# Merge gates as Tanh and inverse deviations as one power on GpSimd, in a hybrid retention and recurrence layer

## Chip, cores and metric

The kernel runs on one core of one Trainium2 chip. The metric is the device time of one execution in microseconds (us), lower is better. Engines are called as in the profile: PE is TensorE's matrix multiply and PEld its weight load, DVE is VectorE, ACT is ScalarE, POOL is GpSimd, SP is SyncE, which only issues transfers here.

## What is computed

One layer on 1024 rows of 1024 features, all in float32 (norm weights, biases and the small gates left out of this sketch):

```python
h = rms_norm(x, norm1_w)
q, k, v, g_ret, x_lru, y_lru, gate_ret, gate_lru = split(h @ w_in)     # 8192 columns
o = head_group_norm(chunkwise_retention(rotary(q), rotary(k), v), ret_gn_w)
y_a = (o * silu(g_ret)) @ w_ret_o
y_b = (rg_lru(conv4(x_lru)) * gelu(y_lru)) @ w_lru_o
mix = sigmoid(gate_ret + merge_gate_b[0]) * y_a + sigmoid(gate_lru + merge_gate_b[1]) * y_b
x = x + mix @ w_out
gate, val = split(rms_norm(x, norm2_w) @ ffn_w_up)                      # 2 * 3072 columns
x = x + (gelu(conv3(gate)) * val) @ ffn_w_down
return rms_norm(x, norm_f_w)
```

`rms_norm` multiplies by `rsqrt(mean(x*x) + 1e-6)`, `head_group_norm` by `rsqrt(var + 1e-6)` for each of four heads. In `rg_lru`, r and i are Sigmoids of two block products, `a = exp(-8 r softplus(-lam))`, and the input of the scan is `sqrt(1 - a*a) * i * x`.

## The kernel before

Every large product is split into three passes of a high and a low part (`split`: ACT rounds a tile to its high part, DVE subtracts for the low part), and many blocks go through a seven-product scheme in place of eight (`mm_fast`, L518), which needs sums of weight blocks and of operand blocks made on DVE. The rest goes through `mm_first` (L494 and L423), `mm_by` (L463) and `mm_std`. A PE instruction is 128x128 weights against 512 columns.

The work is a list of jobs, in the order given by `SEQ`: the projection's column groups, with merge gates (`g`), Gelu branches (`y`), the four retention heads (`h`) and recurrence inputs (`x`) mixed, then the two branch outputs (`ojobs`), `w_out` (`wjobs`), 24 up-projection jobs (`ups`) and twelve down-projection jobs (`djobs`). While a job's matmuls are issued, `pump` prepares weight blocks ahead, `build` prepares operands, and `advance` runs generators of other work (retention, recurrence, rotary tables) a little at a time. These amounts are counted in the program text. The order of instructions on each engine is made by the framework from priorities (`hp`) and from when operands should be ready, so that the small instructions of one chain stand between others.

What the change touches:

- `rstd_of` makes 1/sqrt of a few columns: a Sqrt on ACT, then on DVE a reciprocal and one Newton step of four instructions. It is called by `rms_scale` (first norm, twice with four columns), `retention_head` (eight times with four columns), `out_post` (second norm, four times with two columns) and `final` (last norm, eight times with one column). Its result scales tiles on DVE or ACT right behind it.
- `emit_gate` scales a gate by the row's 1/rms and takes the Sigmoid on ACT with the bias column of `par`, then stores it in `sg_d`. There are 32 such tiles, and SEQ places 12 of them before the first head and 20 behind the last head, among the recurrence blocks (five jobs of four tiles).
- `emit_ret_o` and `emit_lru_o` multiply a bank of the branch product (or the tile that holds it) by the gate read back from `sg_d`, 16 tiles each, and `emit_lru_o` adds the two branches.
- `lru_block` (recurrence) uses Sigmoid, Tanh, Exp and Sqrt on ACT in each half of each of its four blocks.
- `ret_out` multiplies a head's normalized output by `ret_gn_w` and the swish gate.
- ACT needs the function's table in place; a load is put ahead of an activation whose function is not in the table loaded last. Copies, Squares and Identity need no particular one.

GpSimd issues the transfers of the rotary tables and of the up-projection's results (`ff_d`), and makes four constants.

Of the kernel before, what the change touches and what calls it, by code (L numbers as in the profile page):

```python
# [13 lines left out]
F32 = mybir.dt.float32  # L14
F32R = mybir.dt.float32r
I32 = mybir.dt.int32
AF = mybir.ActivationFunctionType
ALU = mybir.AluOpType

P = 128  # L20
# [159 lines left out]
def tile_trunk_layer(ctx, tc, x, xt, positions, params, consts, normf, w_in, w_ro, w_lo,  # L180
# [32 lines left out]
    def pc(name, i):  # L213
        return par[:, PCOL[name] + i:PCOL[name] + i + 1]
# [393 lines left out]
    st = pool.tile([P, 16], F32, tag="st", name="st")  # L608
    nst = pool.tile([P, 5, 8], F32, tag="nst", name="nst")

    def rstd_of(dst, var, tmp):
        S.activation(tmp, var, AF.Sqrt)
        V.reciprocal(dst, tmp)
        V.tensor_mul(tmp, dst, dst)
        V.tensor_mul(tmp, tmp, var)
        V.tensor_scalar(tmp, tmp, -0.5, 1.5, ALU.mult, ALU.add)
        V.tensor_mul(dst, dst, tmp)

    def rms_scale(tiles, n, o=0):

        for t in range(n):
            for c in range(2):
                j = psa.get()
                if c == 0:
                    S.activation(j, tiles[t, c], AF.Square, accum_out=nst[:, c, o + t:o + t + 1])
                else:
                    V.scalar_tensor_tensor(j, tiles[t, c], 1.0, tiles[t, c], ALU.mult, ALU.mult,
                                           accum_out=nst[:, c, o + t:o + t + 1])
                psa.put(j)
        a, b, v, r, w = (nst[:, i, o:o + n] for i in range(5))  # L630
        V.tensor_add(v, a, b)
        V.tensor_scalar(v, v, 1.0 / D, EPS, ALU.mult, ALU.add)
        rstd_of(r, v, w)
        return r

    def reads(fetch, keys, ahead):
# [254 lines left out]
    def lru_block(n, xl):  # L891
        wg = []
        for g in range(2):
            wr = get()
            SY.dma_start(wr, w_gate[n, g])
            wg.append(split(wr))
            put(wr)
            yield 0.6
        carry = {}
        for h in range(2):  # L900
            xc, xs = [], []
            for m in range(2):
                ch = 2 * n + m
                c = get()
                src = xl[m, h]
                S.activation(c, src, AF.Identity, bias=pc("lru_conv_b", ch), scale=pc("lru_conv_w", 24 + ch))
                for s in (1, 2, 3):
                    yield 0.6
                    w = pc("lru_conv_w", 8 * (3 - s) + ch)
                    V.scalar_tensor_tensor(c[:, s:], src[:, :TH - s], w, c[:, s:], ALU.mult, ALU.add)  # L910
                    if h == 1:
                        V.scalar_tensor_tensor(c[:, :s], tails[:, m, 4 - s:4], w, c[:, :s], ALU.mult, ALU.add)
                if h == 0:
                    V.tensor_copy(tails[:, m, :], src[:, TH - 4:])
                put(src)
                xc.append(c)
                xs.append(split(c))
                yield 0.6
            yield from rest()
            rr, ii, th = [], [], []  # L920
            for m in range(2):
                for g, bn, dst in ((0, "lru_b_r", rr), (1, "lru_b_i", ii)):
                    ps = psa.get()
                    q = 0
                    for k in range(2):
                        cs = slice(256 * k + 128 * m, 256 * k + 128 * m + 128)
                        for a, b in PASSES:
                            PE.matmul(ps, wg[g][a][:, cs], xs[k][b], start=q == 0, stop=q == 5)  # L928
                            q += 1
                    t = get()  # L930
                    S.activation(t, ps, AF.Sigmoid, bias=pc(bn, 2 * n + m))
                    psa.put(ps)
                    dst.append(t)
                    yield 0.8
            drop(xs[0])
            drop(xs[1])
            for m in range(2):
                t = get()
                S.activation(t, rr[m], AF.Tanh, scale=lhalf[:, 2 * n + m:2 * n + m + 1])
                V.tensor_mul(ii[m], ii[m], xc[m])  # L940
                put(xc[m])
                th.append(t)
                yield 0.6
            for m in range(2):
                S.activation(rr[m], rr[m], AF.Exp, scale=lneg[:, 2 * n + m:2 * n + m + 1])
            for m in range(2):
                V.scalar_tensor_tensor(rr[m], rr[m], 1.0, th[m], ALU.add, ALU.mult)
                V.tensor_scalar(rr[m], rr[m], -1.0, 1.0, ALU.mult, ALU.add)
                yield 1.0
            for m in range(2):  # L950
                S.activation(th[m], th[m], AF.Sqrt)
            for m in range(2):
                ch = 2 * n + m
                e, i, r = rr[m], ii[m], th[m]
                y = get()
                ST.dma_start(y, y_d[ch, :, TH * h:TH * h + TH])
                V.tensor_mul(i, i, r)
                yield 0.6
                V.scalar_tensor_tensor(i, e, 1.0, i, ALU.add, ALU.mult)
                yield 0.6  # L960
                V.tensor_tensor_scan(r, e, i, 0.0 if h == 0 else carry[m], ALU.mult, ALU.add)
                if h == 0:
                    k = st[:, m:m + 1]
                    V.tensor_copy(k, r[:, TH - 1:TH])
                    carry[m] = k
                V.tensor_mul(y, y, r)
                ST.dma_start(u_d[ch, :, TH * h:TH * h + TH], y)
                put(e, i, r, y)
                yield 1.7
        for w in wg:  # L970
            drop(w)
# [35 lines left out]
    def retention_head(hd, qk, vv):  # L1007
        cur = 0
        mask = cst[:, C_MASK + 128 * hd:C_MASK + 128 * hd + 128]
        for h in range(2):  # L1010
# [48 lines left out]
                V.bn_aggr(mv[:, b, :], bst[:, b, :])  # L1059
                yield 1.5  # L1060
            V.tensor_scalar(rs[:, 0, :], mv[:, :, 1], cst[:, C_GEPS + hd:C_GEPS + hd + 1], None, ALU.add)
            rstd_of(rs[:, 1, :], rs[:, 0, :], rs[:, 2, :])
            for b in range(4):
                o = ob[h, b // 2][:, 256 * (b % 2):256 * (b % 2) + 256]
                V.tensor_scalar(o, o, mv[:, b, 0:1], rs[:, 1, b:b + 1], ALU.subtract, ALU.mult)
# [27 lines left out]
    def ret_out(hd, gg):  # L1093
        yield from rest()
        for h in range(2):
            for m in range(2):
                ps = psa.get()
                for b in range(4):
                    c0 = 256 * (b % 2) + 128 * m
                    PE.transpose(ps[:, 128 * b:128 * b + 128], ob[h, b // 2][:, c0:c0 + 128], ident)  # L1100
                g = gg[m, h]
                V.scalar_tensor_tensor(g, ps, pc("ret_gn_w", 2 * hd + m), g, ALU.mult, ALU.mult)
                psa.put(ps)
                ST.dma_start(og_d[2 * hd + m, :, TH * h:TH * h + TH], g)
                put(g)
                yield 0.8
            put(ob[h, 0], ob[h, 1])
        if hd == HEADS - 1:
            put(*rot.values())


    def emit_gate(which, n):
        def emit(m, h, src, unit):
            t = get() if unit is None else unit

            def go():
                S.activation(t, t, AF.Sigmoid, bias=pc("merge_gate_b", 8 * which + 2 * n + m))
                ST.dma_start(sg_d[which, 2 * n + m, :, TH * h:TH * h + TH], t)
                put(t)
            scaled(t, src, h, go)  # L1120
        return emit
# [51 lines left out]
    def emit_ret_o(n):  # L1173
        def emit(m, h, ps, unit):
            ch = 2 * n + m
            t = ojobs[n].take(m, h)
            V.tensor_mul(t, ps, t)
            ST.dma_start(t1_d[ch, :, TH * h:TH * h + TH], t)
            put(t)
            if unit is not None:  # L1180
                put(unit)
        return emit

    def emit_lru_o(n):
        def emit(m, h, ps, unit):
            ch = 2 * n + m
            g, t = ojobs[4 + n].take(m, h)
            V.tensor_mul(g, ps, g)
            V.tensor_add(t, t, g)
            put(g)  # L1190
            ST.dma_start(mix_d[2 * h:2 * h + 2, :, ch // 4, :, ch % 4, :].rearrange("t m p c -> p (t m) c"),
# [67 lines left out]
    jobs += ojobs  # L1259
    V.memset(st, 1.0)  # L1260
    V.memset(ones, 1.0)
    S.activation(st[:, 0:1], st[:, 1:2], AF.Sqrt)
    queue.extend(jobs)
    SY.dma_start(par, params)
    xs = {}
# [29 lines left out]
    def between(h):  # L1295
        if h == 0:
            for k in range(KT):
                x_set(k, 1, xs[k, 1])
            for _ in range(4):
                next(state["prep"])  # L1300
            SY.dma_start(cst, consts)
# [45 lines left out]

    def out_post(t):
        def fn():
            a, b, v, r, w = (nst[:, i, 2 * t:2 * t + 2] for i in range(5))  # L1350
            V.tensor_add(v, a, b)
            V.tensor_scalar(v, v, 1.0 / D, EPS, ALU.mult, ALU.add)
            rstd_of(r, v, w)
            if t >= 2:
                return norm_half(t - 2)
        return fn
# [183 lines left out]
        V.tensor_mul(fin[m, c], fin[m, c], nf[c])  # L1540

    def final(t, m):
        a, b, v, r, w = (nst[:, i, 2 + m:3 + m] for i in range(5))
        V.tensor_add(v, a, b)
        V.tensor_scalar(v, v, 1.0 / D, EPS, ALU.mult, ALU.add)
        rstd_of(r, v, w)
        r0 = 512 * m + 128 * t
        for c in range(2):
            o = fin.pop((m, c))
# [87 lines left out]
```

## Time and profile before

| | |
|---|---|
| median of 3 runs | 1637.76 us (1635.31 to 1641.26) |
| profiled execution, its own time | 1636.49 us |
| its span, first to last instruction | 1634.7 us |
| granted TensorE clock | 0.999 |
| PE busy | 1607.7 us |
| DVE, ACT, POOL busy | 1325.7, 911.4, 40.6 us |

A line such as L518 is a line of the kernel; nearly all DVE and ACT instructions are recorded under L136, a helper, so they are told apart by tiles: `u` are the general 128x512 tiles, `w` the weight tiles, `g` and `a` PSUM banks, `nst` and `rs` the small tiles of the norms, `st` a scratch column, `par` the parameter columns, `lt` the recurrence's constants, `cst` constants with the identity. An ACT instruction from `u` and `par` to `u` may be a gate or a convolution's first term; one from `u` to `u` is a Gelu, Silu, Sin or a recurrence root; one from `u` and `lt` to `u` is the recurrence's Tanh or Exp; one from `a` and `par` to `u` between 430 and 730 us is one of the recurrence's Sigmoids. Idle time stands in brackets behind an instruction, with what ended it.

### The profile page before, as it was taken

The numbers are of one execution on the slowest core, as the hardware profiler recorded it, in microseconds if no ns is written. First come the engines' busy times: TensorE is split into PE (matmuls) and PEld (weight loads), VectorE is DVE, ScalarE is ACT, GpSimd is POOL, SyncE is SP. The second block draws the span as 40 slices with busy tenths as digits, with TensorE's granted clock in tenths as the row PEclk, the third lists the DMA queues.
The fourth block names the chain that finished last, engine by engine and source line by source line (L and its number), as shares of the span: only waits on it lengthen the run. The fifth ranks groups of instructions, "written<-read, shape, count | busy, mean of one in ns | idle before, by whom it ended". The sixth has DMA issues, their size and how long they took to land.

```text
span 1634.7 us, 21521 instructions
## 1 busy us (share of the span) xinstructions
PE 1607.7 (98%) x7164; PEld 1315.9 (80%) x7164; DVE 1325.7 (81%) x2430; ACT 911.4 (56%) x1545; POOL 40.6 (2%) x60
## 2 busy tenths in 40 slices
PE   8999999999999999999999999999999999999997
PEld 6788888888787878778878778888888888888886
DVE  8998768686898888968878799777777777878895
ACT  7574544445477778763345675444444445553653
POOL 0001000000000000000000001000000000000000
PEclk9999999999999999999999999999999999999999
DMA  8253324242333337657797335444444456878752
GB/s 294 66 186 103 110 72 145 55 136 70 123 117 110 126 101 232 229 197 254 239 312 247 119 110 194 141 137 134 142 135 136 148 174 206 292 244 269 266 185 78
DMA packets 151440, 271.10 MB, mean 166 GB/s; under 512 B 16800, under 2 KB 25120, under 8 KB 151328
## 3 DMA queue, kind: packets, MB, share of 16 engines
q1 hardware_dynamic: 147104, 256.09, 48.4%
q0 software_dynamic: 4224, 13.64, 2.1%
q8 instruction: 56, 0.92, 0.3%
q14 instruction: 56, 0.46, 0.1%
HBM read 188.92 MB, written 75.50 MB: 162 GB/s over the span
## 4 chain that ended last, share of the span: by engine, by line
PE 52%; DVE 9%; ACT 3%; DMA 3%; issue 2%; SPq 0%; DVEq 0%; ACTq 0%
PE g L518 43%; PE g L463 7%; DVE u L136 4%; DVE w L136 2%; DVE u L153 2%; PE a L928 1%; ACT u L136 1%; ACT L136 1%; DMA x_d<-u 1%; DMA w<-mix_d 1%; PE a L1381 0%; ACT w L136 0%; DMA u<-x_d 0%; DMA w<-ff_d 0%; ACT u L153 0%
## 5 line engine op out<-in xcount | busy, mean ns | idle before, releaser
L518 PE MATMUL g<-u,w 128*128 128x512 f32 x5544 | 1294.4, 392 | 3.9 <-ACT u L136 3.1
L518 PEld LDWEIGHTS g<-u,w 128*128 128x128 f32 x5544 | 1034.6, 188 | 222.9 <-ACT u L136 7.4
L136 DVE TENSOR_TENSOR w<-w,w 128x512 fp32r<-128x512 f32 (+1 forms) x766 | 519.6, 688 | 80.0 <-ACT w L136 54.2
L136 ACT CAST w<-w 128x512 fp32r<-128x512 f32 x502 | 309.7, 621 | 379.9 <-PE g L518 269.2
L136 DVE TENSOR_TENSOR u<-u,u 128x512 f32<-128x512 f32 (+1 forms) x411 | 278.8, 690 | 93.0 <-ACT u L136 65.3
L136 DVE TENSOR_TENSOR u<-g,u 128x512 f32<-128x512 f32 x260 | 178.5, 688 | 66.9 <-PE g L518 50.2
L136 ACT COPY u<-g 128x512 f32<-128x512 f32 x242 | 140.2, 581 | 130.6 <-PE g L518 122.3
L463 PE MATMUL g<-u,w 128*128 128x512 f32 x768 | 181.5, 391 | 0.0
L463 PEld LDWEIGHTS g<-u,w 128*128 128x128 f32 x768 | 143.2, 188 | 30.2 <-ACT u L136 0.8
L153 DVE TENSOR_TENSOR u<-u,u 128x512 fp32r<-128x512 f32 (+1 forms) x216 | 139.6, 688 | 1.7 <-ACT u L153 1.5
L136 DVE SCALAR_TENSOR_TENSOR u<-u,par,u 128x511 f32<-128x511 f32 (+4 forms) x220 | 134.4, 632 | 6.9 <-ACT u L136 6.2
L153 ACT CAST u<-u 128x512 fp32r<-128x512 f32 x184 | 104.1, 620 | 35.7 <-DVE u L153 15.8
L136 ACT ACTIVATE u<-u,par 128x512 f32<-128x512 f32 (+1 forms) x116 | 87.4, 772 | 46.1 <-DVE u L136 44.7
L136 ACT ACT_TABLE_LOAD x77 | 98.8, 1283 | 2.1 <-PEq L1629 0.7
L136 ACT ACTIVATE u<-u 128x512 f32<-128x512 f32 x98 | 61.6, 632 | 15.5 <-DVE u L136 15.2
L1432 POOL DMA_DIRECT2D ff_d<-u x48 | 36.1, 752 | 1226.3 <-DVE u L136 1216.5
L928 PE MATMUL a<-u,u 128*128 128x512 f32 x192 | 50.8, 400 | 4.5 <-ACT u L136 2.8
L136 ACT ACTIVATE u<-a,par 128x512 f32<-128x512 f32 (+1 forms) x64 | 41.6, 687 | 13.1 <-PE a L928 7.8
L928 PEld LDWEIGHTS a<-u,u 128*128 128x128 f32 x192 | 34.6, 188 | 16.7 <-ACT u L136 6.5
L136 ACT ACTIVATE a<-u 128x512 f32<-128x512 f32 x40 | 24.0, 600 | 29.2 <-DVE u L136 23.1
L136 DVE SCALAR_TENSOR_TENSOR u<-u,u 128x512 f32<-128x512 f32 x46 | 31.6, 690 | 9.8 <-ACT u L136 9.2
L136 ACT COPY u<-a 128x256 f32<-128x256 f32 (+1 forms) x34 | 13.1, 385 | 37.5 <-PE a L1041 34.9
(74 smaller groups left out, 513.0 us busy)
## 6 DMA issues: line engine op xcount, KB each, us to landing
w<-w_in SPq DMA_DIRECT2D x112, 256.0 KB, 2.6
w<-w_up SPq DMA_DIRECT2D x96, 256.0 KB, 2.7
u<-w_dn SPq DMA_DIRECT2D x88, 256.0 KB, 3.2
u<-x_d SPq DMA_DIRECT2D x60, 256.0 KB, 4.4
x_d<-u SPq DMA_DIRECT2D x48, 256.0 KB, 3.4
ff_d<-u POOLq DMA_DIRECT2D x48, 256.0 KB, 2.9
td_d<-u SPq DMA_DIRECT2D x48, 256.0 KB, 3.5
w<-ff_d SPq DMA_DIRECT2D x48, 256.0 KB, 3.8
```

The costliest lines, as they stand in the source:

```text
L136: ins = fn(*args, **kw)
L153: ins = fn(*args, **kw)
L463: PE.matmul(banks[m, h], jb.blk[an][a][:, c], o[b], start=left[m, h] == 2 and n == 0, stop=left[m, h] == 1 and n == 11)
L518: PE.matmul(bank, w[a][:, c], need(op, (bn, j))[b], start=first and n == 0, stop=n == 11, skip_group_check=True)
L928: PE.matmul(ps, wg[g][a][:, cs], xs[k][b], start=q == 0, stop=q == 5)
L1432: G.dma_start(ff_d[g, 4 * h:4 * h + 4, kh, :, kk, :].rearrange("t p c -> p t c"), c.rearrange("p (t c) -> p t c", t=4))
```

## The change

The gate is written as half of (1 + Tanh of half the argument): `emit_gate` stores the Tanh, the products add 1 before they multiply, and the factor of one half is moved into the recurrence's root (`scale=0.25` inside the Sqrt) and into a halved copy of `ret_gn_w`. `hb` holds the halves of the merge biases and of `ret_gn_w`. `rstd_of` becomes one power with exponent -0.5 on GpSimd, from a tile `half` that holds -0.5. The first activation of the program, which only brings a table, is a Tanh in place of a Sqrt.

```diff
+    half = pool.tile([P, 8], F32, tag="half", name="half")
+    hb = pool.tile([P, 24], F32, tag="hb", name="hb")
+
-    def rstd_of(dst, var, tmp):
-        S.activation(tmp, var, AF.Sqrt)
-        V.reciprocal(dst, tmp)
-        V.tensor_mul(tmp, dst, dst)
-        V.tensor_mul(tmp, tmp, var)
-        V.tensor_scalar(tmp, tmp, -0.5, 1.5, ALU.mult, ALU.add)
-        V.tensor_mul(dst, dst, tmp)
+    def rstd_of(dst, var):
+        G.tensor_tensor(dst, var, half[:, 0:var.shape[-1]], ALU.pow)
+
+    def hc(name, i):
+        j = i + {"merge_gate_b": 0, "ret_gn_w": 16}[name]
+        return hb[:, j:j + 1]
...
-                S.activation(th[m], th[m], AF.Sqrt)
+                S.activation(th[m], th[m], AF.Sqrt, scale=0.25)
...
-            rstd_of(rs[:, 1, :], rs[:, 0, :], rs[:, 2, :])
+            rstd_of(rs[:, 1, :], rs[:, 0, :])
...
-                V.scalar_tensor_tensor(g, ps, pc("ret_gn_w", 2 * hd + m), g, ALU.mult, ALU.mult)
+                V.scalar_tensor_tensor(g, ps, hc("ret_gn_w", 2 * hd + m), g, ALU.mult, ALU.mult)
...
-                S.activation(t, t, AF.Sigmoid, bias=pc("merge_gate_b", 8 * which + 2 * n + m))
+                S.activation(t, t, AF.Tanh, bias=hc("merge_gate_b", 8 * which + 2 * n + m), scale=0.5)
...
-            V.tensor_mul(t, ps, t)
+            V.scalar_tensor_tensor(t, t, 1.0, ps, ALU.add, ALU.mult)
...
-            V.tensor_mul(g, ps, g)
+            V.scalar_tensor_tensor(g, g, 1.0, ps, ALU.add, ALU.mult)
...
-    S.activation(st[:, 0:1], st[:, 1:2], AF.Sqrt)
+    V.memset(half, -0.5)
+    S.activation(st[:, 0:1], st[:, 1:2], AF.Tanh)
...
+            o = PCOL["merge_gate_b"]
+            V.tensor_scalar(hb, par[:, o:o + 24], 0.5, None, ALU.mult)
```

The calls in `rms_scale`, `out_post` and `final` lose their third operand in the same way.

More of the change, by code (lines that the diff above doesn't have):

```diff
@@ L629, in rms_scale @@
                 psa.put(j)
-        a, b, v, r, w = (nst[:, i, o:o + n] for i in range(5))
+        a, b, v, r = (nst[:, i, o:o + n] for i in range(4))
         V.tensor_add(v, a, b)
         V.tensor_scalar(v, v, 1.0 / D, EPS, ALU.mult, ALU.add)
-        rstd_of(r, v, w)
+        rstd_of(r, v)
         return r
@@ L1349, in fn @@
         def fn():
-            a, b, v, r, w = (nst[:, i, 2 * t:2 * t + 2] for i in range(5))
+            a, b, v, r = (nst[:, i, 2 * t:2 * t + 2] for i in range(4))
             V.tensor_add(v, a, b)
             V.tensor_scalar(v, v, 1.0 / D, EPS, ALU.mult, ALU.add)
-            rstd_of(r, v, w)
+            rstd_of(r, v)
             if t >= 2:
@@ L1542, in final @@
     def final(t, m):
-        a, b, v, r, w = (nst[:, i, 2 + m:3 + m] for i in range(5))
+        a, b, v, r = (nst[:, i, 2 + m:3 + m] for i in range(4))
         V.tensor_add(v, a, b)
         V.tensor_scalar(v, v, 1.0 / D, EPS, ALU.mult, ALU.add)
-        rstd_of(r, v, w)
+        rstd_of(r, v)
         r0 = 512 * m + 128 * t
```

## The prediction

> **What bounds the kernel now.** I read the page first, then busy time by stage, then what TensorE (PE) waited for.
>
> ```profile
> span 1634.7 us, 21521 instructions
> PE 1607.7 (98%) x7164; PEld 1315.9 (80%) x7164; DVE 1325.7 (81%) x2430; ACT 911.4 (56%) x1545; POOL 40.6 (2%) x60
> L136 ACT ACT_TABLE_LOAD x77 | 98.8, 1283 | 2.1 <-PEq L1629 0.7
> ```
>
> PE is busy for 98% of the span, so whatever leaves ScalarE (ACT) or VectorE (DVE) is worth only what PE waits for them. ACT spends 98.8 us on 77 table loads, which looks large and is the obvious hope. The stages say where PE could still gain. Columns: window, its length, busy us (and instructions) of PE, weight loads, DVE, ACT, GpSimd (POOL), then granted clock, DMA share, GB/s.
>
> ```profile
> core 0: us, PE busy (x) PEld busy (x) DVE busy (x) ACT busy (x) POOL busy (x), PEclk, DMA share, GB/s
> 0.00:60.00 60.00, 53.77 (x221) 43.26 (x222) 51.39 (x110) 42.53 (x81) 0.20 (x4) 1.00 0.65 227
> 60.00:140.00 80.00, 80.00 (x351) 65.40 (x350) 78.53 (x165) 52.75 (x80) 4.30 (x8) 1.00 0.45 145
> 140.00:430.00 290.00, 287.35 (x1369) 236.50 (x1368) 213.58 (x464) 133.29 (x238) 0.00 (x0) 1.00 0.31 97
> 430.00:730.00 300.00, 295.54 (x1291) 239.83 (x1290) 256.13 (x438) 227.86 (x329) 0.00 (x0) 1.00 0.47 155
> 730.00:960.00 230.00, 227.37 (x1024) 184.78 (x1023) 188.51 (x329) 117.81 (x221) 0.77 (x1) 1.00 0.68 223
> 960.00:1400.00 440.00, 439.83 (x1939) 363.03 (x1938) 350.95 (x585) 223.12 (x379) 35.31 (x47) 1.00 0.49 158
> 1400.00:1635.00 235.00, 223.84 (x981) 183.08 (x979) 186.63 (x345) 114.00 (x222) 0.00 (x0) 0.99 0.64 216
> ```
>
> ```profile
> PE g L494 <- ACT u L136: 5.6, 1, 5.6
> PE g L518 <- ACT u L136: 3.1, 5, 1.3
> PE a L928 <- ACT u L136: 2.8, 3, 1.6
> PE a L928 <- DVE u L136: 1.6, 3, 0.9
> PE a L1039 <- DVE sm L136: 1.5, 1, 1.5
> PE a L1381 <- ACT a L136: 0.9, 1, 0.9
> ```
>
> ```profile
> 1620.25 5.73 PE L518 MATMUL g<-u,w 128*128 128x512 f32 x24 [0.68 <-ACT u L136]
> ```
>
> The second fence names PE's waits (total, times, longest). The first, 5.6 us, is the start: the first weights arrive, and the change leaves that alone. The last matmuls end at 1620.25 + 5.73 = 1625.98, so 8.72 us of the span is the tail behind PE. Idle PE per stage is length minus busy: 6.23 (0.6 without the start), 0.00, 2.65, 4.46, 2.63, 0.17, and 11.16 less 0.30 beyond the span's end and 8.72 of tail, 2.14. Together 12.7 us. That, and whatever the tail gives, is nearly all the change can win. A busy PE can still be slowed: from 960 to 1400 it issues 1939 matmuls in 440 us, one per 0.227 us; at that pace the 1291 of the stage from 430 to 730 (all of 512 columns) would take 293 us, so 7 us of that stage is lost rather than 4.46.
>
> **Table loads, stage by stage.** The change removes 22 roots from ACT (two for the first norm, eight in retention, four for the second norm, eight for the last) and turns 32 gate Sigmoids into Tanhs. These are the loads from 60 to 140, 140 to 430 and 430 to 730 us, in that order.
>
> ```profile
> L136 ACT ACT_TABLE_LOAD x10 | 12.8, 1283 | 0.2
> L136 ACT ACT_TABLE_LOAD x16 | 20.5, 1283 | 0.3
> L136 ACT ACT_TABLE_LOAD x48 | 61.6, 1283 | 0.9
> ```
>
> Stage 60 to 140, 12 gates mixed with Gelus: a Gelu sends a load ahead of itself and the next gate another.
>
> ```profile
> 87.25 1.28 ACT L136 ACT_TABLE_LOAD   x1
> 88.54 0.63 ACT L136 ACTIVATE u<-u 128x512 f32<-128x512 f32 x1
> 575.59 1.26 ACT L136 ACTIVATE u<-a,par 128x512 f32<-128x512 f32 x2 [1.55 <-PE a L928]
> 576.75 0.72 ACT L136 ACTIVATE u<-u,lt 128x512 f32<-128x512 f32 x1
> 577.49 1.28 ACT L136 ACT_TABLE_LOAD   x1
> ```
>
> The last three rows show a Tanh (576.75) behind two Sigmoids without a load, and a load only ahead of the Exp: Tanh lies in Sigmoid's table. Whether it lies in Gelu's no row shows, so after the change this stage has 2 loads (Gelu, Sin) if it does and 10 if not; I take 2, eight fewer, 10.3 us of ACT. Worth on the path: nothing, since PE idles 0.00 us there.
>
> Stage 140 to 430: the eight retention roots stand between Silus, a load into the root and one back. One load for Silu stays: 15 fewer, 19.2 us of ACT. PE's 2.65 us there are, by the named waits, on DVE (1.5 us of it for the masked scores), and DVE is busy 213.58 of 290. I take zero, with 1.5 us as the other end.
>
> Stage 430 to 730: 20 gates stand between pieces of the recurrence, which still needs Sigmoid, Tanh, Exp and a root of its own in every half.
>
> ```profile
> 599.31 1.28 ACT L136 ACT_TABLE_LOAD   x1
> 602.00 0.73 ACT L136 ACTIVATE u<-u,par 128x512 f32<-128x512 f32 x1 [1.40 <-DVE u L136]
> ```
>
> Here the load before the gate (behind a recurrence root) also serves the recurrence's next Sigmoids. A Tanh needs a load behind a root just the same; if that brings the table that Tanh shares with Exp, the next Sigmoid needs a further one. Four gate groups follow a root, so 48 loads become 48 at best and 52 otherwise; I take 52, that is 5.1 us more of ACT. What of it is felt comes from the chain of waits, cut to this stage:
>
> ```profile
> by line: DVE u L136 16.8%; PE g L518 15.6%; PE g L463 9.3%; PE a L928 8.4%; DVE w L136 6.3%; ACT L136 4.2%; ACT u L136 4.1%; issue 3.8%; ACT w L136 1.5%; DVE u L153 1.2%; DMA u<-y_d 1.1%; SPq L1152 0.1%; DVE st L136 0.1%; DVEq L136 0.1%; DV
> ```
>
> "ACT L136" without a tile is the table loads: 4.2% of the 290 us that the chain covers here is 12.2 us, a fifth of the 61.6 us. A fifth of 5.1 is +1.0 us; ends 0 and +5.1. One more load, ahead of the last norm's roots, goes as well: 77 - 8 - 15 + 4 - 1 = 57 loads.
>
> The Trainium skill, "ScalarE: Activation LUTs", section "What ACT_TABLE_LOAD costs", gives a switch as 1283 ns for the load and some 1380 ns of drain, 2.66 us in all. The trace agrees on the load and not on the drain: the Gelu of 88.54 starts 1.29 us after the load of 87.25. By that rule the 20 loads saved would be an estimated 53 us of ACT, by the rows 26.
>
> **The power in place of the root.** Each root's chain is one ACT root and five small DVE instructions; the retention chain's are
>
> ```profile
> L136 DVE TENSOR_TENSOR rs<-rs x24: 155/161/164, 179.3 to 428.9; 128x4 f32<-128x4 f32 x24
> ```
>
> so DVE loses 22 x 5 x 0.161 = 17.7 us and ACT 22 x 0.19 = 4.2 (root row below). GpSimd gets 22 powers. No row has one. The nearest GpSimd rows are a memset of one column and a DMA issue:
>
> ```profile
> L1432 POOL DMA_DIRECT2D ff_d<-u x48 | 36.1, 752 | 1226.3 <-DVE u L136 1216.5
> L1629 POOL MEMSET const-float32-1.0<- 128x1 f32 x1 | 0.1, 98 | 0.0
> ```
>
> A power computes and a memset only stores, so I take the upper row, 0.75 us, and keep 0.1 below and four times the upper row, 3.0 us, above. Only where a root is last on the path does it matter. The tail:
>
> ```profile
> 1628.45 0.15 DVE L136 TENSOR_SCALAR nst<-nst 128x1 f32<-128x1 f32 x1
> 1628.76 0.19 ACT L136 ACTIVATE nst<-nst 128x1 f32<-128x1 f32 x1
> 1628.97 0.17 DVE L136 RECIPROCAL nst<-nst 128x1 f32<-128x1 f32 x1 [0.37 <-ACT nst L136]
> 1629.95 0.72 ACT L136 ACTIVATE u<-u,nst 128x512 f32<-128x512 f32 x1 [1.00 <-DVE nst L136]
> ```
>
> From the variance (1628.60) to its use (1629.95) is 1.35 us; the two crossings between engines take 0.16 and 0.02. With a power: 0.18 + 0.75 = 0.93, a gain of 0.4 us (1.07 with a memset's price, a loss of 1.8 with 3.0). The second norm's last two roots lie on the same kind of chain toward h2, where 0.9 of PE's waits is on ACT at the transposes: I give them 0.3 together, ends +1.07 x 2 and -1.8 x 2. The other roots have cover. The first norm's, the tightest for DVE (78.53 of 80 from 60 on):
>
> ```profile
> 39.87 0.17 DVE L136 TENSOR_SCALAR nst<-nst 128x4 f32<-128x4 f32 x1
> 44.79 0.17 DVE L136 COPY rcol<-nst 128x4 f32<-128x4 f32 x1
> ```
>
> Other DVE work fills the 4.75 us between the variance and the copy that uses it. A DVE that stands at that copy keeps the weight splits queued behind it waiting, and PE waits for those; a power of up to 4.75 us is hidden. GpSimd's own queue has only DMA issues; the sine-table ones come after the first powers, those of the up-projection between the second norm's and the last's, so nothing is queued behind a waiting power.
>
> The Trainium skill, "GPSIMD Engine Reference", section "2.1 Instruction dispatch", says that the first call of a freshly loaded kernel pays about 6 us more; no run here shows it. By it the first power would outlast the cover by an estimated 2 us, once.
>
> **Edits at nothing.** The 32 products with a gate become (t + 1) times the bank:
>
> ```profile
> L136 DVE SCALAR_TENSOR_TENSOR u<-u,u 128x512 f32<-128x512 f32 x46 | 31.6, 690 | 9.8 <-ACT u L136 9.2
> L136 DVE TENSOR_TENSOR u<-g,u 128x512 f32<-128x512 f32 x260 | 178.5, 688 | 66.9 <-PE g L518 50.2
> ```
>
> 690 against 688 ns, nothing even without cover. Halved constants cost two small DVE instructions before 60 us; scales in ScalarE instructions that ran anyway cost nothing.
>
> **Sum**, against the profiled execution of 1636.5 us: tail -0.4, second norm -0.3, recurrence +1.0, all else 0: 1636.8. The profiled execution lies 1.3 below the median of the runs shown, well within their spread, so I state 1637.0: no change that can be told. Over or under 0.3% (4.9 us) is what a measurement of this kernel can tell.
>
> **Rivals.**
> *Freed engines feed PE better (faster).* For it: nearly all PE's waits are on ACT or DVE. Against it: most loads go where PE does not wait. If the waits on DVE at the scores (1.5), on ACT at the transposes (0.9) and those of L518 on ACT (3.1) go, with 0.4 in the tail: 1636.5 - 5.9 = 1630.6. 16%.
> *More loads in the recurrence (slower).* Place: 430 to 730 us, ACT busy 227.86 of 300 and on the chain. If all 52 loads or more come, each on the chain (5.1), and the saved 0.7 elsewhere does not show: 1641.6, and 1643 with a fifth group. It decides once the stage has over 51 loads and PE's idle time there is over 8 us. 11%.
> *DVE stands behind slow powers (slower).* Past 1.17 us (1.35 less crossings) a power costs its excess in the tail and twice at the second norm; at 3.0 us that is 5.5: 1642.0. 6%.
> *A new order.* The order on each engine follows priorities and readiness, and 110 DVE and 42 ACT instructions fewer shift it; four new waits like the longest (1.6 each) cost 6.4, four that vanish bring as much: 1630 or 1643. 7%, of it 5 slower.
> *The loads do not fall* (Tanh shares no table with Gelu): still 1637, as the early stage hides them; it is within the forecast.
>
> **Numbers.** Forecast 60%. Faster: 16 + 2 = 18%. Slower: 11 + 6 + 5 = 22%. The range takes in 1630.6 below and 1643 above with a little for the spread: 1629 to 1645.
>
> **What would show it.** Right: 55 to 60 loads, one or two from 140 to 430, 50 or so from 430 to 730; DVE near 1308 and ACT near 880 busy; PE idle still 0 from 60 to 140 and 4 to 5.5 in the recurrence; 0.8 to 1.1 us from the last variance to its use. Wrong: PE's idle sum outside start and tail far from 12.7, powers beyond 1.2 us, or a stage whose matmuls are spread further apart.

## The result and the profile after

The changed kernel takes 1642.83 us (median of 12 runs, 1640.19 to 1646.87) against 1637.74 us of the kernel before (12 runs, 1635.31 to 1641.44): a ratio of 1.0030 with a 95% interval of 1.0021 to 1.0039, so 5.1 us slower. The time lies inside the stated range of 1629 to 1645, but the forecast was no change. The profiled execution took 1642.95 us, its span is 1641.2 us, 6.5 us more than before, and its granted clock 0.997. In code, lines after the edit stand two to five lower: the key transposes of retention are L1002 (L1000 before), the scores' products L1041, the transposes of `ret_out` L1102 (L1100), the recurrence's block products L930, the second norm's transposes L1386. The power itself is L615.

The page's totals:

```profile
span 1641.2 us, 21420 instructions
PE 1608.0 (98%) x7164; PEld 1317.8 (80%) x7164; DVE 1313.3 (80%) x2322; ACT 882.8 (54%) x1503; POOL 60.2 (4%) x82
L136 ACT ACT_TABLE_LOAD x57 | 73.1, 1283 | 1.7 <-PEq L1634 0.7
```

ACT lost 28.6 us of work and DVE 12.4, and 20 table loads are gone. PE's busy time is the same within 0.3 us. So nearly all of the 6.5 us must stand as idle time of PE (a stretch of slowed matmuls counts as busy; one comes below), and the table by stage has it:

```profile
0.00:60.00 60.00, 52.75 (x221) 42.85 (x222) 51.21 (x103) 43.08 (x80) 3.01 (x6) 1.00 0.66 227
60.00:140.00 80.00, 80.00 (x351) 65.46 (x350) 76.69 (x161) 41.25 (x70) 4.31 (x8) 1.00 0.48 145
140.00:430.00 290.00, 284.63 (x1349) 234.47 (x1348) 206.48 (x423) 111.20 (x213) 8.08 (x8) 0.99 0.32 94
430.00:730.00 300.00, 293.99 (x1283) 238.25 (x1282) 253.72 (x432) 231.88 (x331) 0.00 (x0) 1.00 0.49 156
730.00:960.00 230.00, 226.92 (x1025) 185.46 (x1024) 185.94 (x309) 114.32 (x209) 3.98 (x5) 1.00 0.69 221
960.00:1400.00 440.00, 439.38 (x1936) 362.69 (x1935) 350.04 (x582) 222.96 (x378) 33.80 (x45) 1.00 0.50 155
```

Length minus PE's busy time, against the same stage before: +1.02, 0, +2.72, +1.55, +0.45, +0.45, together 6.2 of the 6.5 us. The largest share falls in the retention stage, from 140 to 430 us, where POOL now shows eight powers; and 0.96 of the 1.55 us behind it is still retention's, a wait of the fourth head's transposes that falls at 432.40 us. The waits of PE that name DVE, in retention and, in the last row, at the second norm (total, times, longest):

```profile
PE a L1102 <- DVE u L136: 3.0, 4, 1.0
PE a L1002 <- DVE u L136: 2.0, 1, 2.0
PE a L1041 <- DVE sm L136: 1.3, 3, 0.9
PE a L1386 <- DVE u L136: 0.6, 1, 0.6
```

The L1102 row had no counterpart among the waits before. The trace of the first head shows what makes it (start, length, engine, instruction, idle time before it and what ended that):

```profile
200.54 0.22 DVE L136 TENSOR_SCALAR rs<-mv,cst 128x4 f32<-128x4 f32 x1
200.91 1.01 POOL L615 TENSOR_TENSOR rs<-rs,half 128x4 f32<-128x4 f32 x1 [19.39 <-DVE rs L136]
201.86 1.04 PE L1102 MATMUL a<-cst,u 128*128 128x128 f32 x8
201.95 1.38 DVE L136 TENSOR_SCALAR u<-u,mv,rs 128x256 f32<-128x256 f32 x4 [1.19 <-POOL rs L615]
202.66 0.71 PE L518 MATMUL g<-u,w 128*128 128x512 f32 x2
203.25 0.75 DVE L136 SCALAR_TENSOR_TENSOR u<-a,hb,u 128x512 f32<-128x512 f32 x1
204.05 0.66 PE L1102 MATMUL a<-cst,u 128*128 128x128 f32 x4 [0.68 <-DVE u L136]
```

DVE hands the variance to POOL at 200.76, does nothing for 1.19 us until the power is there, scales the second half's four blocks (1.38 us), and only then, at 203.25, makes the product that empties the first half's PSUM bank. PE has by then issued eight transposes (201.86), two big products, and stands 0.68 us for that bank; it happens once in each of the four heads. The same place in the kernel before:

```profile
198.95 1.04 PE L1100 MATMUL a<-cst,u 128*128 128x128 f32 x8
199.59 0.75 DVE L136 SCALAR_TENSOR_TENSOR u<-a,par,u 128x512 f32<-128x512 f32 x1 [0.65 <-PE a L1100]
199.75 5.73 PE L518 MATMUL g<-u,w 128*128 128x512 f32 x24
204.37 0.16 DVE L136 TENSOR_TENSOR rs<-rs 128x4 f32<-128x4 f32 x1
205.60 0.41 PE L1100 MATMUL a<-cst,u 128*128 128x128 f32 x2
```

There the product ran on DVE at 199.59, right behind the transposes of 198.95, the Newton step's instructions lay between other DVE work until 204.37, and 24 big products (5.73 us) stood between the first half's transposes and the second half's. So the power did two things: it put a gap into DVE's queue, and it moved the second half's transposes up until they met that gap.

The second place is the key transposes at 152.81 us, in the same stage:

```profile
151.47 0.69 DVE L136 TENSOR_TENSOR w<-w,w 128x512 fp32r<-128x512 f32 x1
152.07 2.62 DVE L136 TENSOR_TENSOR u<-u,u 128x512 f32<-128x512 f32 x4
152.81 0.66 PE L1002 MATMUL a<-cst,u 128*128 128x128 f32 x4 [2.05 <-DVE u L136]
```

They wait 2.05 us (0.85 before), because weight operations stand between the rotary sums that they need (the last of them at 151.47); before, DVE made five of those sums in a row from 150.08:

```profile
150.08 3.23 DVE L136 TENSOR_TENSOR u<-u,u 128x512 f32<-128x512 f32 x5
152.03 0.66 PE L1000 MATMUL a<-cst,u 128*128 128x128 f32 x4 [0.85 <-DVE u L136]
```

Two windows of the changed kernel's trace, one behind this wait and one undisturbed (the last columns are POOL, clock, DMA share, GB/s):

```profile
153.00:158.00 5.00, 5.00 (x20) 4.05 (x20) 2.26 (x4) 1.37 (x2) 0.00 (x0) 0.66 0.00 0
240.00:245.00 5.00, 5.00 (x24) 4.20 (x24) 3.13 (x8) 1.20 (x3) 0.00 (x0) 1.00 0.00 0
```

Behind the wait the granted clock is 0.66 over 5 us, which is 3.4 us at half speed, and PE issues 20 matmuls where the undisturbed 5 us hold 24. Half speed for 3.4 us is worth up to 1.7 us beside the wait. Counted by PE's matmuls in order of their starts, the changed kernel is 0.03 us behind the kernel before at the 614th and 2.83 us behind at the 634th: 1.2 us of that is the longer wait, 1.6 us the slow stretch.

### The profile page after: what moved, and what is told of

It is laid out like the page before. It is cut to its first block, busy times and chain, and to the rows that moved or that the text cites. A ratio compares the mean times of both kernels' runs of the same rounds, so it can differ in the third digit from the quotient of the medians.

```text
span 1641.2 us, 21420 instructions
## 1 busy us (share of the span) xinstructions
PE 1608.0 (98%) x7164; PEld 1317.8 (80%) x7164; DVE 1313.3 (80%) x2322; ACT 882.8 (54%) x1503; POOL 60.2 (4%) x82
## 4 chain that ended last, share of the span: by engine, by line
PE 52%; DVE 7%; ACT 3%; issue 3%; DMA 1%; SPq 0%; POOL 0%; POOLq 0%; DVEq 0%; ACTq 0%
PE g L518 43%; PE g L463 8%; DVE u L136 4%; DVE w L136 2%; PE a L930 1%; DVE u L153 1%; ACT u L136 1%; ACT L136 1%; ACT u L153 1%; DMA u<-x_d 1%; ACT w L136 1%; DMA w<-mix_d 0%; DMA w<-ff_d 0%; DMA x_d<-u 0%; PE a L1386 0%
## 5 line engine op out<-in xcount | busy, mean ns | idle before, releaser
L136 DVE TENSOR_TENSOR u<-u,u 128x512 f32<-128x512 f32 (+1 forms) x402 | 272.0, 688 | 94.1 <-ACT u L136 64.8
L136 DVE TENSOR_TENSOR u<-g,u 128x512 f32<-128x512 f32 x237 | 162.7, 688 | 64.1 <-PE g L518 50.1
L136 ACT ACTIVATE u<-u,par 128x512 f32<-128x512 f32 (+1 forms) x84 | 64.7, 791 | 25.3 <-DVE u L136 24.9
L930 PE MATMUL a<-u,u 128*128 128x512 f32 x192 | 50.8, 400 | 5.1 <-ACT u L136 3.2
L930 PEld LDWEIGHTS a<-u,u 128*128 128x128 f32 x192 | 34.6, 188 | 17.8 <-ACT u L136 7.8
L136 DVE SCALAR_TENSOR_TENSOR u<-u,u 128x512 f32<-128x512 f32 x55 | 37.7, 689 | 9.7 <-ACT u L136 9.3
L615 POOL TENSOR_TENSOR nst<-nst,half 128x1 f32<-128x1 f32 (+2 forms) x14 | 11.4, 817 | 777.7 <-DVE nst L136 777.7
L136 ACT ACTIVATE u<-u,hb 128x512 f32<-128x512 f32 x32 | 22.9, 723 | 27.7 <-DVE u L136 27.5
```

What stands on the lines that cost most here:

```text
L136: ins = fn(*args, **kw)
L615: G.tensor_tensor(dst, var, half[:, 0:var.shape[-1]], ALU.pow)
```

## The experiments

All were measured beside the kernel before on the same chip, 10 to 12 executions each unless said otherwise; the medians of before were 1637.32 us for the first four kernels, 1636.32 for the next three and the last, and 1635.98 for the powers of the second and last norm and for the second profile of two powers. My theory from the traces above: the loss is the powers', not the gates', and mostly those of two places, retention and the first norm. The rivals: the gates' loads in the recurrence, and a general shift of order to which everything adds a little.

**The gates alone and the powers alone.** Two kernels split the change in its halves.

```diff
# gates alone: the change with the old roots
-        G.tensor_tensor(dst, var, half[:, 0:var.shape[-1]], ALU.pow)
+        S.activation(tmp, var, AF.Sqrt)
+        V.reciprocal(dst, tmp)
+        ...
# powers alone: the change with the old gates
-                S.activation(t, t, AF.Tanh, bias=hc("merge_gate_b", 8 * which + 2 * n + m), scale=0.5)
+                S.activation(t, t, AF.Sigmoid, bias=pc("merge_gate_b", 8 * which + 2 * n + m))
```

> Only the gates as Tanh; all 22 roots as before. Two theories for the 5 us that the change lost. (1) The order: with a power in retention the transposes of a head's second half stand two products behind the first half's, where they stood 24 behind before, and PE waits there for DVE (3.0 us); with a power in the first norm the key transposes of the first head are waited for (2.0 us instead of 0.8, with slowed matmuls behind). (2) The gates: four more table loads in the recurrence, 52 for 48, on its chain, PE idle there 6.0 us for 4.5. By (1) this kernel is within 2 us of before (ratio 0.999 to 1.001) and PE does not wait at the second half's transposes. By (2) it shows most of the loss: 1.002 to 1.003, PE idle near 6 us from 430 to 730 us.

> Only the powers, all 22 of them; the gates stay Sigmoids. By the order theory the whole loss shows: ratio 1.0025 to 1.0035, the waits at the second half's transposes 3 us in sum, the first key transposes near 2 us. By the gates theory it is level with before, 0.999 to 1.001.

Gates alone: 1637.76 us, ratio 1.0006 (0.9995 to 1.0017). Powers alone: 1641.95 us, 1.0027 (1.0018 to 1.0036). The gates kernel has 75 loads, 53 of them from 430 to 730 us where before had 48, and PE's idle time there is 4.45 us against 4.46: the extra loads in the recurrence cost nothing. The powers kernel has both waits of retention, 3.0 and 1.7 us. The loss is the powers'.

**No power in retention; no power in the first norm.** Each takes the old root, reciprocal and Newton step back at one place of the changed kernel.

```diff
# no power in retention (retention_head)
-            rstd_of(rs[:, 1, :], rs[:, 0, :])
+            root_of(rs[:, 1, :], rs[:, 0, :], rs[:, 2, :])    # root_of: the old rstd_of
# no power in the first norm (rms_scale)
-        rstd_of(r, v)
+        root_of(r, v, w)
```

> The change with the eight retention roots back as Sqrt, reciprocal and Newton step; powers elsewhere, gates as Tanh. By the order theory about 3 us come back against the change (ratio to before 1.0010 to 1.0018), the waits at the second half's transposes are gone, the wait at the first key transposes stays near 2 us, and the Silu loads return (73 loads, 19 us more ACT) at no cost. By the gates theory nothing comes back: 1.0025 to 1.0035.

> The change with the two roots of the first norm back as Sqrt, reciprocal and Newton step; powers elsewhere, gates as Tanh. By the order theory the wait at the first key transposes falls from 2.0 us to about 0.8 without slowed matmuls behind it and the one near 45 us from 1.3 to about 0.7: 2 to 3.5 us come back (ratio 1.0008 to 1.002), the 3 us at the second half's transposes stay. By the gates theory 1.0025 to 1.0035.

Without the retention power: 1640.32 us, 1.0015 (1.0005 to 1.0025); the waits at the transposes of `ret_out` fall from 3.0 us to 0.13. The key transposes still wait, in the trace of this kernel:

```profile
153.72 0.66 PE L1010 MATMUL a<-cst,u 128*128 128x128 f32 x4 [2.48 <-DVE u L136]
```

and the window behind them shows the clock fall again:

```profile
153.90:158.90 5.00, 5.00 (x20) 4.05 (x20) 2.26 (x4) 1.38 (x2) 0.00 (x0) 0.66 0.00 0
```

Without the first norm's power: 1639.99 us, 1.0018 (1.0010 to 1.0027); the key transposes wait 0.9 us again, and the 3.0 us at `ret_out` stay. A wait of L423 for ACT at 45.06 us, 1.33 us in the changed kernel and 0.67 before, is gone too. This profile has its slow stretch elsewhere, behind a wait of 2.03 us in the recurrence (668 us). Each of the two powers thus carries its own wait and, by the ratios against 1.0030, 0.0015 and 0.0012 of the time, 2.5 and 2.0 us; the intervals of about 0.001 to either side leave the sizes rough. A power in the first norm, at 39.5 us, delays a transpose at 152 us: it does so through the order of DVE's work, and which instruction there tips that order I have not found.

**Later transposes.** This keeps all powers and makes the second half of `ret_out` stand back, so that some 24 big products lie between the halves as before (22 at the first head of its trace).

```diff
         for h in range(2):
+            if h == 1:
+                yield from rest(2)
             for m in range(2):
                 ps = psa.get()
```

> The change, with one line more: the generator of a head's output pauses for two rests before its second half, which puts the second half's transposes 24 products behind the first half's, where they stood before, for 2 after. All 22 powers stay. If the order is what costs in retention, the waits at those transposes (3.0 us) vanish and about 3 us come back against the change: ratio to before 1.0010 to 1.0018, like the kernel without powers in retention. If the power's own latency costs, wherever the transposes stand, the ratio stays 1.0025 to 1.0035.

1640.44 us, 1.0022 (1.0012 to 1.0032). The waits at `ret_out` go from 3.0 to 0.3 us, with all powers in place: the waits come from the order read above. But only some 1.3 us came back of the time, less than I expected, and the two intervals overlap, so the times alone don't show a gain: PE now idles 7.07 us in the recurrence (6.01 in the changed kernel, 5.05 without the fourth head's wait), with waits of 1.67 us at 646.87 and 2.20 us at 721.4, and the clock is at 0.69 in the 5 us behind the latter. The key transposes still wait, 2.33 us, with a slow stretch behind them. What was gained in one stage was in part lost again in the next.

**Both mended.** Later transposes, and the old root in the first norm.

> The pause before the second half's transposes and the first norm's roots back as Sqrt with Newton step; powers in retention, the second and the last norm, gates as Tanh. If the two costs are separate and add up, both come back: ratio to before 0.9995 to 1.0008, PE waits at the second half's transposes 0 and at the first key transposes 0.9 us. If one wait only moves elsewhere, 1.0015 or more.

1637.38 us, 1.0004 (0.9994 to 1.0015), level with before. In its trace, the order of PE at the first head is that of the kernel before:

```profile
198.47 1.03 PE L1112 MATMUL a<-cst,u 128*128 128x128 f32 x8
199.26 5.70 PE L518 MATMUL g<-u,w 128*128 128x512 f32 x24
204.81 1.03 PE L1112 MATMUL a<-cst,u 128*128 128x128 f32 x8
```

No wait stands in front of either group; two of the later heads still wait, 1.3 us together, where the changed kernel had 3.0, and the key transposes wait 1.1 us. The power stays in retention here, and once almost nothing meets it the loss is not to be seen.

**The retention power twice.** A second, equal power ahead of the first, 1 us more for everything that waits for it.

```diff
+            rstd_of(rs[:, 2, :], rs[:, 0, :])
             rstd_of(rs[:, 1, :], rs[:, 0, :])
```

> The change with each retention power taken twice (the first one's result goes unused): 1.0 us more on GpSimd before DVE may go on, the order on PE is that of the change. If PE waits at the second half's transposes for DVE, which stands for the power, each of the four waits grows by 0.9 to 1.0 us, 3.0 to 7 us in sum, and the time by 3.5 to 5 us: ratio to before 1.005 to 1.006. If the transposes wait for something else (a bank, the weights), nothing grows: 1.003.

1651.55 us (six runs), 1.0087 (1.0068 to 1.0105). In its trace, at the first head:

```profile
200.61 1.98 POOL L615 TENSOR_TENSOR rs<-rs,half 128x4 f32<-128x4 f32 x2 [19.05 <-DVE rs L136]
202.62 1.38 DVE L136 TENSOR_SCALAR u<-u,mv,rs 128x256 f32<-128x256 f32 x4 [2.16 <-POOL rs L615]
204.72 0.66 PE L1103 MATMUL a<-cst,u 128*128 128x128 f32 x4 [1.64 <-DVE u L136]
```

The added 0.97 us of power appears whole in DVE's idle time (1.19 to 2.16) and whole in PE's wait (0.68 to 1.64): the power is on the path at each head, as the theory says. The waits at `ret_out` sum to 6.9 us, 3.9 more than in the changed kernel. The median grew by more than that, 8.7 us over the changed kernel. The profiled run was the fastest of the six, 1646.17 us at a mean clock of 0.999; the other five took 1649.22 to 1655.51, four of them at 0.996 or 0.997. So the same kernel was profiled once more, with one time.

> The kernel with the retention power taken twice, looked at once more, since its time grew by more than its waits in the one profile. If the rest lies in drops of TensorE's clock, this profile shows a lower granted clock in windows of a few us behind the ret_out transposes' waits (1.6 us each); if the waits differ from run to run, the ret_out transposes wait for more than 6.9 us in all.

1648.65 us at a mean clock of 0.996. The sum of waits at `ret_out` is 6.9 us again, so it does not differ between these two. The clock does. The first window is of this run, the second of the earlier one, both behind the fourth head's transposes, which had waited 1.93 us in each:

```profile
435.00:440.00 5.00, 5.00 (x19) 4.15 (x20) 3.19 (x5) 0.00 (x0) 0.00 (x0) 0.66 0.57 216
```

```profile
436.90:441.90 5.00, 5.00 (x27) 4.22 (x28) 4.53 (x9) 1.55 (x3) 0.00 (x0) 1.00 0.70 249
```

19 matmuls against 27 in the same 5 us. The recurrence's L930 also waited longer, 4.0 us against 2.5, one of it 2.23 us with another drop to 0.66. Drops of the clock behind waits near 2 us are therefore part of the excess. An estimate from the mean clocks: 0.996 in place of 0.999 over 1650 us is some 10 us more at half speed, three such stretches, worth up to 5 us; the clocks are given to 0.001, so this is rough, and it does not explain the run of 1649.22 us, whose clock was 0.999.

**The powers of the second and last norm alone**, with the gates: the old roots both in retention and in the first norm.

> The change, but with the first norm and the retention norms on root, reciprocal and Newton step again; the powers stay in the second and the last norm, and the gates stay Tanh. Theory (the loss is the retention power's and the first norm's power's; the second norm's power costs PE 0.5 to 0.9 us, and the tail gives nothing): 1.0000 to 1.0010, with the ret_out transposes' wait on DVE back near 0.4 us, the key transposes' near 0.9 us, and the second norm's transposes still waiting 0.5 us at about 939 us. Rival (every power costs about alike, by standing on another engine): half of the loss stays, 1.0015 or more.

1637.57 us, 1.0006 (0.9995 to 1.0018). The waits at `ret_out` are gone from the list, the key transposes wait 1.2 us, the second norm's 0.6 us stay. Without the two powers named, the change is level with before. Its interval still reaches the 1.0015 of the rival that every power costs about alike; what speaks against that rival is the kernel with both mended, which keeps 20 of the 22 powers and is level with before.

**The tail alone.** The kernel before with a power in the last norm only, and the last half's scalings on DVE where ACT had them, to let ACT take its next Square early.

```diff
-        rstd_of(r, v, w)
+        G.tensor_tensor(r, v, half, ALU.pow)
...
-            if (m, c) == (0, 1):
+            if m == 1 or c == 1:
                 V.tensor_scalar(o, o, r, None, ALU.mult)
```

> The kernel before with powers in the last norm alone, and the first of each last pair's scalings (rows of m = 1) on DVE, so that ACT is free for the last Square. Gates, retention and the other norms as before. From the last matmul's end to the end of the span 8.7 us become 7.9 to 8.2: ratio to before 0.9990 to 0.9998. If the scalings on DVE only push back the last products there, 1.000.

1636.11 us, 0.9996 (0.9988 to 1.0005): not told from before. Its trace says why:

```profile
1623.76 0.55 POOL L1548 TENSOR_TENSOR nst<-nst,half 128x1 f32<-128x1 f32 x1 [12.73 <-DVE nst L136]
1624.35 0.88 DVE L136 TENSOR_SCALAR u<-u,nst 128x512 f32<-128x512 f32 x2 [0.73 <-POOL nst L1548]
1625.14 0.69 DVE L136 TENSOR_TENSOR u<-g,u 128x512 f32<-128x512 f32 x1
```

The two scalings (1624.35) now stand on DVE in front of the last sum of product and residual (1625.14), for which PE had been done at 1623.81. From PE's end to the span's end it is 9.4 us, not the 8.7 of before. My edit moved the obstacle from ACT to DVE.

## Why the prediction was wrong

**What held.** The loads came out as counted, 57, with 2 from 60 to 140 us and 1 from 140 to 430; ACT at 882.8 us (forecast 880) and DVE at 1313.3 (1308; it fell by 12.4 us where I had counted 17.7). PE's idle time from 60 to 140 stayed at 0. The 10 us of loads saved there and the 19 in retention bought nothing that shows, as said. The 22 powers took 0.89 us on average, against an estimate of 0.75: 0.54 to 1.00 us on one column, 0.70 to 1.07 on two, 1.01 to 1.03 on four in retention, and 1.39 and 1.42 for the two of the first norm, beyond the 1.2 us that I had named as a sign of being wrong. The other sign came too: PE's idle time outside start and tail is 18.6 us, where 12.7 had been. The edits at nothing cost nothing: gates alone are level.

**Recurrence, forecast +1.0.** In the changed kernel PE's idle time there rose by 1.55 us, but 0.96 of it is the wait of the fourth head's transposes, so the recurrence has 0.6; with the gates alone, and more loads, it rose by nothing. So the term was nearly of the right size, by luck: the loads on which it rested cost nothing. Without the fourth head's wait, the six profiles with both Tanh gates and powers in retention have 4.46 to 7.07 us there and the six others, before included, 3.93 to 5.14. These overlap, and what makes the 0.6 is open.

**Retention, forecast 0: the step that failed.** The sentence "Only where a root is last on the path does it matter" and "The other roots have cover" looked for cover as time between the variance and its use. In retention that time was there: the old chain ran for 6.6 us beside other DVE work. But it was cover made by the order of that one program. With five DVE instructions gone, the order brought the scalings and the transposes up to the power, and DVE stood with nothing to fill its gap and with the bank's release queued behind. I had named the mechanism ("a DVE that stands at that copy keeps the weight splits queued behind it waiting") and weighed it only for the first norm; the rival of slow powers had it at the tail and the second norm, from 1.17 us of price on. Here a power of 1.01 us decided, at a place for which that rival had no threshold. It cost 3.0 us of waits, and 2.5 us of time by the kernel without it.

**First norm, forecast 0.** The cover failed here too. The copy that uses the power was pulled forward, from 44.79 us to 40.96, and DVE stood in front of it:

```profile
40.96 0.17 DVE L136 COPY rcol<-nst 128x4 f32<-128x4 f32 x1 [0.91 <-POOL nst L615]
```

PE's wait at 45.06 us is 0.67 us longer than before and gone without this power. The larger part was the rival "a new order", which I gave 7%: a wait grown by 1.2 us at 152.81 and the clock's drop behind it, 2.0 us by the kernel without that power. I had priced a new order by waits alone, 1.6 us each. A wait with a drop of the clock behind it costs up to 1.7 us more.

**Second norm, forecast -0.3.** The way from variance to use did get shorter. But the scalings, and with them the transposes, moved to a place where PE was due, as the trace of the changed kernel shows:

```profile
938.00 0.70 POOL L615 TENSOR_TENSOR nst<-nst,half 128x2 f32<-128x2 f32 x1 [25.61 <-DVE nst L136]
938.73 1.68 DVE L136 TENSOR_SCALAR u<-u,nst 128x512 f32<-128x512 f32 x4 [0.81 <-POOL nst L615]
939.27 0.44 PE L1386 MATMUL a<-cst,u 128*128 128x128 f32 x2 [0.56 <-DVE u L136]
```

0.56 us of wait in place of a gain, too little to be seen in a time.

**Tail, forecast -0.4.** From the last variance (1635.99) to its use it takes 0.72 us instead of 1.35, a gain of 0.63. It was eaten, in the trace just ahead:

```profile
1632.49 0.54 POOL L615 TENSOR_TENSOR nst<-nst,half 128x1 f32<-128x1 f32 x1 [13.10 <-DVE nst L136]
1633.06 1.33 ACT L136 ACTIVATE u<-u,nst 128x512 f32<-128x512 f32 x2 [1.73 <-POOL nst L615]
1634.30 0.58 ACT L136 ACTIVATE a<-u 128x512 f32<-128x512 f32 x1
```

The tile before the last gets its power so early that ACT's two scalings (1633.06) go ahead of the last tile's Square (1634.30), which the end waits for. PE's end lies 8.7 us ahead of the span's end, as before.

Taken together, the terms of the sum that I had put at zero for order (retention, first norm) are 4.5 of the 5.1 us by the kernels that leave out one of them, and 3.9 by the one that leaves out both; the priced terms (recurrence, second norm, tail) came out within a microsecond each and decided nothing.

## What to carry to other kernels

Time between a value and its use is cover only as long as the order stays. Where a planner orders the engines, ask what a shorter chain will pull forward, and what stands behind the engine that then has to wait: here a PSUM bank's release. A chain of small instructions spread between others can hide better than one quicker instruction on another engine, for which the consumer's queue stands still. And when an engine at 98% sets the time, a count of what the others save says nothing: here 41 us saved on two engines came with 5 us lost.

## What was not expected of the hardware

The TensorE clock fell to half for about 3.4 us behind single waits of about 2 us. It fell behind waits of 2.05 (changed kernel), 2.48 (no power in retention), 2.03 (no power in the first norm, at 668 us), 2.33 and 2.20 (later transposes), 2.23 and 1.93 us (two powers, second profile); it did not behind waits of 2.07 and 1.93 us in the first profile of two powers, nor behind 1.6 us in the kernel before (666 us, window at 1.00).

The traces' records of the clock show what lies behind this. Each of the seven drops lasts 3.413 us and begins a whole number of such pieces after the first record of full speed: 42 pieces at the key transposes in three kernels, 193, 208, 125 and 196 in the others. Cut into these pieces, PE's idle time in the piece just ahead of a drop is 1.93 to 2.47 us; in every other piece of the twelve traces, up to the last matmul, it is 1.72 us or less. The two long waits without a drop were cut by a border, 2.07 us into 0.88 and 1.18, 1.93 us into 0.36 and 1.57. So in these traces it is the idle time within one piece that decides, somewhere between 1.72 and 1.93 us, and where a wait falls among the pieces differs between runs of one kernel.

The Trainium skill, "TensorE: Matmul & The Clock Gate", Part 1, tells of a free-running window of about 3.4 us by whose activity the clock is halved or restored, and warns of idle gaps above that length; the traces agree on the window and its length, but gaps well below it, from 1.93 us, were enough here.

A power with a column of exponents cost GpSimd 0.54 to 1.00 us on one column and 1.0 to 1.4 us on four; the program's first took 1.39 us, its second, also of the first norm, 1.42, so nothing extra fell on the first call.
